# Hybrid decoder layer: the channel mixer's up projection in seven block products instead of eight, the down projection's running sums in DRAM

## The chip, the cores and the metric

The kernel runs on one core of one Trainium2 chip. Its time is device microseconds of one launch. The profile is one execution, taken by the hardware profiler; its times are microseconds (us) from the first instruction unless marked ns. The engines are PE (TensorE matmul), PEld (TensorE weight load), DVE (VectorE), ACT (ScalarE), POOL (GpSimd) and SP (SyncE, which here only issues DMAs).

## The reference

One decoder layer over 2048 tokens of 1024 features, in float32. A first part (a gated linear attention and a recurrent head group) ends in a residual stream x; the change leaves it alone. The second part is the channel mixer:

```python
h = modulate(x, norm_ffn_g, sh_f, sc_f)              # RMS norm, scale, shift
u = h @ w_up                                         # 1024 -> 5632 columns
up = pad(u, 2 tokens in front)
u = sum(conv_w[j] * up[:, j:j + T] for j in range(3)) + conv_b
gate, val = split(u, 2)                              # 2816 columns each
x = x + gt_f * ((silu(gate) * val) @ w_down)         # 2816 -> 1024
out = rms_norm(x, final_g)
```

## The kernel before

Features lie on the 128 partitions and tokens on the free axis. Tokens go in four blocks of 512. Phase 1 computes the first part. Phase 2 is the channel mixer: it takes two token blocks at a time (a pass; HB = 2, so there are two passes), and in each pass goes over the 22 pairs of a gate tile and a value tile, of 128 hidden features each.

Every float32 matrix product is made of three matmuls on rounded operands: a tensor t is split into hi (a copy that rounds, on ScalarE) and lo = t - hi (a subtraction on VectorE or GpSimd), and the product is hi·hi + hi·lo + lo·hi. A matmul takes 128 features of weights (128x128) against 512 tokens. `gemm3` (L276 to L278) sums the eight blocks of 128 features of one tile and one token block in a PSUM bank: 24 matmuls. `Weights` loads and splits weights (L179 the hi part on ScalarE; L182 the lo part, on GpSimd for every third piece and on VectorE otherwise).

For a tile, `conv_tile` runs `gemm3` for both token blocks, copies the bank to SBUF (`ub`, L1121), and applies the three taps (L1123 to L1125, with the last two tokens of the block before in `ccar`). `hidden` makes silu(gate)·value of two such tiles and splits it (`hh`, `hl`, L1151 and L1152). After a group of four or five hidden tiles (`kgroups`), `down` multiplies them into the 8 output tiles of both blocks (L1162 to L1164) and adds to `acc`, 16 tiles that stay in SBUF for the whole pass (L1167). `finish` normalises the output.

`stage_h` makes a block's operands: 8 tiles, each loaded from `x2d`, scaled (L265), rounded (L266) and subtracted (L267). The operands of the first two blocks are made where phase 1 ends, beside the last steps of the recurrent state's chain (the `rw_` and `rs_` tiles); those of the next two blocks, and the last block's output projection (`d3`, 192 matmuls), at the end of the first pass.

The order of each engine's instructions is fixed when the program is built, by a scheduler that goes by priorities (the order of the code) and by its own estimate of when inputs are ready and buffers free. Each engine then runs its list in order and waits at semaphores. All DMAs are issued from SP's list.

## Time and profile before

| | |
|---|---|
| time, median of 3 runs | 2974.28 us (2970.91 to 2977.05) |
| span of the profiled execution | 2964.6 us |
| PE busy | 2835.6 us (96%) |
| DVE busy | 1879.8 us (63%) |
| ACT busy | 1290.3 us (44%) |
| POOL busy | 735.9 us (25%) |
| mean granted clock of TensorE | 0.975 of full speed |

The span runs from the first to the last instruction. The profiled execution has no time of its own beside its span; the median of the runs lies 9.7 us above the span, which is what lies around it. Busy shares are means over phases with different limits. A matmul's duration overlaps with its neighbours' (they are pipelined), so its rate is read from the distance of two starts. The engine's idle time counts where others wait for it.

### The profile page before, as it was taken

Reading aid. Unit: us, or ns where it says so; the run is one execution under the profiler, and the core shown is the slowest. Engines: PE = TensorE matmul, PEld = TensorE weight load, DVE = VectorE, ACT = ScalarE, POOL = GpSimd, SP = SyncE. Lnnn points to the kernel's source line nnn. Section 1 sums busy time; section 2 is a strip of 40 time slices with the busy share of each in tenths; the row PEclk is TensorE's granted clock in tenths of the full one; section 3 lists DMA queues with packets and bytes.
Section 4 is the critical chain, followed back from the end, with each engine's and each line's share of the span. In section 5 each row is a group of like instructions: output and inputs, shape, how many; then the busy total and the mean of one; then the engine's idle time right before and its main releaser. Section 6 shows DMA issues by size and latency. Waiting matters only on the chain.

```text
span 2964.6 us, 53912 instructions
## 1 busy us (share of the span) xinstructions
PE 2835.6 (96%) x20824; PEld 2310.7 (78%) x20824; DVE 1879.8 (63%) x3877; ACT 1290.3 (44%) x2625; POOL 735.9 (25%) x995
## 2 busy tenths in 40 slices
...
GB/s 280 166 169 191 159 122 136 150 143 117 118 104 109 105 113 150 144 141 105 180 63 55 44 53 42 55 38 62 98 152 161 45 52 38 61 36 56 52 36 79
DMA packets 250050, 309.61 MB, mean 104 GB/s; under 512 B 68160, under 2 KB 139072, under 8 KB 249792
## 3 DMA queue, kind: packets, MB, share of 16 engines
...
q8 instruction: 164, 2.69, 0.4%
...
## 4 chain that ended last, share of the span: by engine, by line
PE 69%; DVE 10%; DMA 5%; ACT 3%; issue 2%; POOL 0%; SPq 0%; DVEq 0%; ACTq 0%; POOLq 0%
PE g_bank L276 13%; PE g_bank L277 13%; PE g_bank L278 13%; PE g_bank L1162 5%; PE g_bank L1164 5%; PE g_bank L1163 5%; DMA w_st<-in_ada_t 1%; PE gl_bank L690 1%; DVE w_lo L182 1%; DMA inv_a<-rw_mab 1%; DVE rw_pr L893 1%; DVE rw_t L832 1%; PE g_bank L444 1%; PE g_bank L442 1%; PE g_bank L443 1%
## 5 line engine op out<-in xcount | busy, mean ns | idle before, releaser
L276 PE MATMUL g_bank<-h_hi,w_hi 128*128 128x512 f32 x2144 | 846.3, 395 | 6.9 <-ACT carry L331 3.6
L277 PE MATMUL g_bank<-h_lo,w_hi 128*128 128x512 f32 x2144 | 844.9, 394 | 1.5 <-DVE h_lo L267 1.5
L278 PE MATMUL g_bank<-h_hi,w_lo 128*128 128x512 f32 x2144 | 844.2, 394 | 0.4 <-DVE w_lo L182 0.4
L179 ACT CAST w_hi<-w_st 128x512 fp32r<-128x512 f32 (+2 forms) x424 | 306.1, 725 | 533.3 <-PE g_bank L1163 310.3
L276 PEld LDWEIGHTS g_bank<-h_hi,w_hi 128*128 128x128 f32 x2144 | 405.3, 189 | 94.6 <-ACT carry L331 4.7
L277 PEld LDWEIGHTS g_bank<-h_lo,w_hi 128*128 128x128 f32 x2144 | 406.0, 189 | 85.8 <-DVE h_lo L267 2.1
L278 PEld LDWEIGHTS g_bank<-h_hi,w_lo 128*128 128x128 f32 x2144 | 405.6, 189 | 85.8 <-DVE w_lo L182 0.9
L182 POOL TENSOR_TENSOR w_lo<-w_st,w_hi 128x512 fp32r<-128x512 f32 (+2 forms) x141 | 228.2, 1619 | 696.0 <-ACT w_hi L179 648.2
L182 DVE TENSOR_TENSOR w_lo<-w_st,w_hi 128x512 fp32r<-128x512 f32 (+2 forms) x283 | 247.0, 874 | 144.0 <-ACT w_hi L179 135.9
L1124 DVE SCALAR_TENSOR_TENSOR cv<-ub,vt,cv 128x512 f32<-128x512 f32 x176 | 151.7, 862 | 229.2 <-ACT cv L1123 226.1
L1167 DVE SCALAR_TENSOR_TENSOR acc<-g_bank,mod,acc 128x512 f32<-128x512 f32 (+1 forms) x168 | 120.9, 723 | 240.1 <-PE g_bank L1164 240.1
L1163 PE MATMUL g_bank<-hl,w_hi 128*128 128x512 f32 x640 | 250.7, 392 | 0.0
L1164 PE MATMUL g_bank<-hh,w_lo 128*128 128x512 f32 x640 | 249.8, 392 | 0.0
L1162 PE MATMUL g_bank<-hh,w_hi 128*128 128x512 f32 x640 | 248.5, 392 | 0.0
L1126 POOL COPY ccar<-ub 128x2 f32<-128x2 f32 x176 | 66.5, 378 | 535.7 <-ACT ub L1121 535.4
L1121 ACT COPY ub<-g_bank 128x512 f32<-128x512 f32 x176 | 102.5, 583 | 103.5 <-PE g_bank L278 94.4
L1151 ACT CAST hh<-th 128x512 fp32r<-128x512 f32 x88 | 54.6, 621 | 209.3 <-DVE th L1147 209.3
L1163 PEld LDWEIGHTS g_bank<-hl,w_hi 128*128 128x128 f32 x640 | 120.1, 188 | 27.0
L1164 PEld LDWEIGHTS g_bank<-hh,w_lo 128*128 128x128 f32 x640 | 120.1, 188 | 27.1
L1162 PEld LDWEIGHTS g_bank<-hh,w_hi 128*128 128x128 f32 x640 | 120.2, 188 | 26.8
L1125 DVE SCALAR_TENSOR_TENSOR cv<-ub,vt,cv 128x512 f32<-128x512 f32 x176 | 134.4, 764 | 5.9
L1123 ACT ACTIVATE cv<-g_bank,vt 128x512 f32<-128x512 f32 x176 | 138.1, 784 | 0.0
...
## 6 DMA issues: line engine op xcount, KB each, us to landing
...
w_st<-in_w_in SPq DMA_DIRECT2D x168, 256.0 KB, 2.9
proj<-ev SPq DMA_DIRECT2D x100, 256.0 KB, 2.9
w_st<-in_ada_t SPq DMA_DIRECT2D x64, 256.0 KB, 3.5
x_k<-in_x SPq DMA_DIRECT2D x48, 256.0 KB, 3.5
w_st<-in_w_out SPq DMA_DIRECT2D x48, 256.0 KB, 3.2
w_st<-in_ffn_down SPq DMA_DIRECT2D x48, 256.0 KB, 2.6
...
```

Of the source, the lines that this page charges most:

```text
L179: A.copy(out=hi[:, 0:w], in_=t[:, 0:w])
L182: eng.tensor_tensor(out=lo[:, 0:w], in0=t[:, 0:w], in1=hi[:, 0:w].bitcast(F32), op=ALU.subtract)
L276: PE.matmul(out=ps, lhsT=wh, rhs=hi, start=k == 0, stop=False)
L277: PE.matmul(out=ps, lhsT=wh, rhs=lo, start=False, stop=False)
L278: PE.matmul(out=ps, lhsT=wl, rhs=hi, start=False, stop=k == KT - 1)
L1123: A.activation(out=cv, in_=ps, func=AF.Identity, scale=vt[:, o_cw + 88 + t:o_cw + 89 + t], bias=vcol("conv_b", t))
L1124: V.scalar_tensor_tensor(out=cv, in0=ub[:, 1:NB + 1], scalar=vt[:, o_cw + 44 + t:o_cw + 45 + t], in1=cv, op0=ALU.mult, op1=ALU.add)
L1125: V.scalar_tensor_tensor(out=cv, in0=ub[:, 0:NB], scalar=vt[:, o_cw + t:o_cw + t + 1], in1=cv, op0=ALU.mult, op1=ALU.add)
L1162: PE.matmul(out=ps, lhsT=wh, rhs=hh, start=j == 0, stop=False)
L1163: PE.matmul(out=ps, lhsT=wh, rhs=hl, start=False, stop=False)
L1164: PE.matmul(out=ps, lhsT=wl, rhs=hh, start=False, stop=j == n - 1)
L1167: V.scalar_tensor_tensor(out=a_, in0=ps, scalar=mod[:, 40 + ft:41 + ft], in1=a_, op0=ALU.mult, op1=ALU.add)
```

## The change

The up projection of a pass is a product of two by two blocks: the rows are the gate tile and the value tile, the inner dimension is cut into a lower and an upper half of 512 features, and the columns are the pass's two token blocks. Eight block products of 12 matmuls became seven (Strassen's scheme in Winograd's form). The weights are a11, a12 (gate, lower and upper features) and a21, a22 (value); the operands b11, b21 are the first block's halves, b12, b22 the second's. For every pair of tiles GpSimd makes four sums of weights (s1, s2, a21 + a11, s2 + a12), and seven pieces are split instead of the two tiles. The operand sums t1 to t4 are made once in a pass, by `operands_b`. The products collect in two banks: x is read four times while products are still added to it, and z twice. The value tile comes out negated; its taps are negated to match (`ncw`). `up_a` makes the first block's gate tile (two products), `up_b` adds three products and yields the second block's value tile, and `up_c`, which is issued after the next pair's `up_a`, adds the last two.

The room that the operands need comes from `acc`: the running sums of the down projection now lie in DRAM (`accd`), and every group loads, adds and stores the 16 tiles through five buffers (`acct`). The groups of hidden tiles are one of two and five of four. The mask and constant tile `ct` moved to another pool without its first 128 columns, and a scratch of the DMA program is smaller. Up to the last steps of phase 1 the engines' lists are the same as before.

```diff
-    pools["np"], pools["nst"], pools["nhl"], pools["nev"], pools["nx"] = 1, 2, 3, 4, 4
+    pools["np"], pools["nst"], pools["nhl"], pools["nev"], pools["nx"] = 2, 8, 4, 6, 5
...
+    def either():
+        turn[0] += 1
+        return G if turn[0] % 3 == 0 else V
+    def split(t, pair):
+        hi, lo = pair
+        A.copy(out=hi, in_=t)
+        either().tensor_tensor(out=lo, in0=t, in1=hi.bitcast(F32), op=ALU.subtract)
...
+    def operands_b(b, hs):
...
+        def put(n_, t):
+            pair = hc(n_)
+            hs[n_].append(pair)
+            split(t, pair)
+        def whole(n_, k):
+            d = ubt()[:, 0:NB]
+            hi, lo = hs[n_][k]
+            either().tensor_tensor(out=d, in0=hi.bitcast(F32), in1=lo.bitcast(F32), op=ALU.add)
+            return d
+        for k in range(4):
+            two = []
+            for q in (k, k + 4):
+                xk = ubt()[:, 0:NB]
+                nc.sync.dma_start(out=xk, in_=x2d[b][:, q, :])
+                V.scalar_tensor_tensor(out=xk, in0=xk, scalar=mod[:, 32 + q:33 + q], in1=rb, op0=ALU.mult, op1=ALU.mult)
+                A.activation(out=xk, in_=xk, func=AF.Identity, bias=mod[:, 24 + q:25 + q])
+                two.append(xk)
+            b12, b22 = two
+            c = ubt()[:, 0:NB]
+            V.tensor_tensor(out=c, in0=b22, in1=b12, op=ALU.subtract)
+            put("t3", c)
+            b11 = whole("b11", k)
+            V.scalar_tensor_tensor(out=c, in0=c, scalar=-1.0, in1=b11, op0=ALU.mult, op1=ALU.subtract)
+            put("t2", c)
+            G.tensor_tensor(out=b12, in0=b11, in1=b12, op=ALU.subtract)
+            put("t1", b12)
+            put("b22", b22)
+            b21 = whole("b21", k)
+            V.scalar_tensor_tensor(out=c, in0=c, scalar=-1.0, in1=b21, op0=ALU.mult, op1=ALU.subtract)
+            put("t4", c)
+        return hs
...
+    def product(ps, t, ops, first, last):
+        wh, wl = parts_of(t)
+        for k in range(4):
+            c = slice(k * P, (k + 1) * P)
+            hi, lo = ops[k]
+            PE.matmul(out=ps, lhsT=wh[:, c], rhs=hi, start=first and k == 0, stop=False, skip_group_check=True)
+            PE.matmul(out=ps, lhsT=wh[:, c], rhs=lo, start=False, stop=False, skip_group_check=True)
+            PE.matmul(out=ps, lhsT=wl[:, c], rhs=hi, start=False, stop=last and k == 3, skip_group_check=True)
...
+    def up_a(j, hs):
+        u = {}
+        gw, vw = ffn_up[j], ffn_up[NH + j]
+        a11, a12, a21, a22 = (raw(w_[:, c * NB:(c + 1) * NB]) for w_ in (gw, vw) for c in range(2))
+        u["x"], w_ = gbank(), gbank()
+        product(u["x"], a11, hs["b11"], True, False)
+        s1, s2 = raw(), raw()
+        G.tensor_tensor(out=s1, in0=a21, in1=a22, op=ALU.add)
+        G.tensor_tensor(out=s2, in0=s1, in1=a11, op=ALU.add)
+        G.tensor_tensor(out=a21, in0=a21, in1=a11, op=ALU.add)
+        u["c11"] = ubt()
+        A.copy(out=u["c11"][:, 2:NB + 2], in_=u["x"])
+        product(w_, a12, hs["b21"], True, True)
+        V.tensor_tensor(out=u["c11"][:, 2:NB + 2], in0=w_, in1=u["c11"][:, 2:NB + 2], op=ALU.add)
+        u["w"] = (a12, a21, a22, s1, s2)
...
+    def up_b(u, hs):
+        a12, a21, a22, s1, s2 = u["w"]
+        product(u["x"], s2, hs["t2"], False, False)
+        u["c21"] = ubt()
+        A.copy(out=u["c21"][:, 2:NB + 2], in_=u["x"])
+        G.tensor_tensor(out=s2, in0=s2, in1=a12, op=ALU.add)
+        u["z"] = gbank()
+        product(u["z"], a21, hs["t3"], True, False)
+        product(u["x"], s1, hs["t1"], False, False)
+        u["c22"] = ubt()
+        A.copy(out=u["c22"][:, 2:NB + 2], in_=u["x"])
+        V.tensor_tensor(out=u["c22"][:, 2:NB + 2], in0=u["z"], in1=u["c22"][:, 2:NB + 2], op=ALU.add)
+    def up_c(u, hs):
+        a12, a21, a22, s1, s2 = u["w"]
+        product(u["x"], s2, hs["b22"], False, True)
+        u["c12"] = ubt()
+        A.copy(out=u["c12"][:, 2:NB + 2], in_=u["x"])
+        product(u["z"], a22, hs["t4"], False, True)
+        V.tensor_tensor(out=u["c21"][:, 2:NB + 2], in0=u["z"], in1=u["c21"][:, 2:NB + 2], op=ALU.add)
...
-            ps = gbank()
-            gemm3(ps, w, h)
...
-    kgroups = ((0, 5), (5, 10), (10, 14), (14, 18), (18, 22))
+    kgroups = ((0, 2), (2, 6), (6, 10), (10, 14), (14, 18), (18, 22))
...
+    def down_group(e, k0, k1, hid):
+        for ft in range(KT):
+            w = parts_of(raw(ffn_down[ft][:, k0 * P:k1 * P], (k1 - k0) * P), (k1 - k0) * P)
+            for i in range(HB):
+                b = e * HB + i
+                a_ = acct()
+                nc.sync.dma_start(out=a_, in_=x2d[b][:, ft, :] if k0 == 0 else accd[b][ft])
+                down(ft, w, hid, i, a_, b)
+                nc.sync.dma_start(out=accd[b][ft], in_=a_)
...
+        for j in range(NH):
+            u = up_a(j, hs)
+            if prev is not None:
+                up_c(prev[1], hs)
+                g = group_of[prev[0]]
+                hid[g].append(hidden(*prev))
+                if prev[0] == g[1] - 1:
+                    ready = g
+            up_b(u, hs)
+            while pending and j > 0:
+                finish(*pending.pop(0))
+            if ready is not None:
+                down_group(e, *ready, hid.pop(ready))
+                ready = None
+            prev = (j, u)
...
+            d3 = stage_d(NBLK - 1, prep_d(NBLK - 1), lp.tile([P, NB], F32, name="d_ss", tag="th", bufs=2))
+            h2 = operands_a((e + 1) * HB)
...
+                if ft == 3:
+                    operands_b((e + 1) * HB + 1, h2)
```

**VectorE where the channel mixer starts.** Before: `x_k` is a loaded tile of the second or first block, `h_lo` its operand, `rw_sv` the recurrent state.

```order
L265 SCALAR_TENSOR_TENSOR x_k<-x_k,mod,rbc 128x512 x4
L182 TENSOR_TENSOR w_lo<-w_st,w_hi 128x1024
L267 SCALAR_TENSOR_TENSOR h_lo<-x_k,mod,h_hi 128x512 x4
L265 SCALAR_TENSOR_TENSOR x_k<-x_k,mod,rbc 128x512
L182 TENSOR_TENSOR w_lo<-w_st,w_hi 128x1024
L1005 TENSOR_TENSOR rw_sv<-rs_bank,rw_sv 64x256 x2
L267 SCALAR_TENSOR_TENSOR h_lo<-x_k,mod,h_hi 128x512
L265 SCALAR_TENSOR_TENSOR x_k<-x_k,mod,rbc 128x512
L1006 TENSOR_TENSOR rw_sv<-rw_sv,rw_ec 64x256 x2
```

After, the second block's operands (`operands_b`): `ub` is scratch, `h_lo` the low part of one of t1, t2, t3, t4 and b22, `w_lo` a split weight.

```order
L1183 TENSOR_TENSOR ub<-ub 128x512
L1170 TENSOR_TENSOR ub<-h_hi,h_lo 128x512
L1139 TENSOR_TENSOR h_lo<-ub,h_hi 128x512
L1178 SCALAR_TENSOR_TENSOR ub<-ub,mod,rbc 128x512
L1186 SCALAR_TENSOR_TENSOR ub<-ub 128x512
L1139 TENSOR_TENSOR w_lo<-w_st,w_hi 128x512
L1031 TENSOR_SCALAR hn_rk<-rj_bank 128x8
L1139 TENSOR_TENSOR h_lo<-ub,h_hi 128x512
L1178 SCALAR_TENSOR_TENSOR ub<-ub,mod,rbc 128x512
L1139 TENSOR_TENSOR w_lo<-w_st,w_hi 128x512
L1183 TENSOR_TENSOR ub<-ub 128x512
L1139 TENSOR_TENSOR h_lo<-ub,h_hi 128x512
```

Two rows for a tile of 128 features became, for a pair of tiles (k and k + 4), two scalings, up to two sums of hi and lo (L1170), the differences (L1183, L1186, L1192) and up to five subtractions (L1139), a part of them on GpSimd. From the first scaling to the last of these operands VectorE's list has 79 rows' worth of instructions, 64 of them with 128x512 elements, and GpSimd's has 23 with 128x512 elements; TensorE's list has 72 matmuls of the up projection ahead of the last operand. At the end of the first pass the same list stands between the `rbc` of the fourth block and its last t operand: 57 VectorE instructions of 128x512, 20 of GpSimd, and 113 matmuls of 128x512.

**GpSimd in the middle of a pass.** Before: `ccar` and `ub` are the two carried tokens, `w_lo` split weights.

```order
L1120 COPY ub<-ccar 128x2 x2
L182 TENSOR_TENSOR w_lo<-w_st,w_hi 128x512
L1126 COPY ccar<-ub 128x2
L182 TENSOR_TENSOR w_lo<-w_st,w_hi 128x512
L182 TENSOR_TENSOR w_lo<-w_st,w_hi 128x1024
L1126 COPY ccar<-ub 128x2
L1120 COPY ub<-ccar 128x2 x2
```

After: `w_st` are raw weights and their sums.

```order
L1224 TENSOR_TENSOR w_st<-w_st 128x512
L1226 TENSOR_TENSOR w_st<-w_st 128x512
L1225 TENSOR_TENSOR w_st<-w_st 128x512
L1139 TENSOR_TENSOR w_lo<-w_st,w_hi 128x512
L1258 COPY ub<-ub 128x2
L1139 TENSOR_TENSOR w_lo<-w_st,w_hi 128x512
L1239 TENSOR_TENSOR w_st<-w_st 128x512
L1224 TENSOR_TENSOR w_st<-w_st 128x512
L1257 COPY ub<-ccar 128x2
L1259 COPY ccar<-ub 128x2
L1226 TENSOR_TENSOR w_st<-w_st 128x512
L1225 TENSOR_TENSOR w_st<-w_st 128x512
```

Between two groups of the down projection the list of TensorE now has 324 matmuls of the up projection in a row; beside them VectorE has 74 instructions of 128x512 (26 taps L1264 and L1265, 18 of the hidden tile L1277, L1278 and L1281, 17 splits, and 13 that read a PSUM bank), GpSimd 22 of 128x512 (13 sums of weights, 9 splits) and 21 copies of two columns. The 192 matmuls of a group follow nearly in one piece.

**SP in a group of the down projection.** Before: only weights are loaded (`acc` is loaded once, at a pass's first group).

```order
L174 DMA w_st<-in_ffn_up 128x1024
L174 DMA w_st<-in_ffn_down 128x640 x8
L174 DMA w_st<-in_ffn_up 128x1024 x10
L174 DMA w_st<-in_ffn_down 128x640 x8
L174 DMA w_st<-in_ffn_up 128x1024 x8
L174 DMA w_st<-in_ffn_down 128x512 x8
```

After: `acc` is a buffer, `acc_3` and the like a running sum in DRAM.

```order
L1330 DMA acc_3_18105<-acc 128x512
L1328 DMA acc<-acc_5_18115 128x512
L1330 DMA acc_3_18113<-acc 128x512
L1328 DMA acc<-acc_6_18108 128x512
L1330 DMA acc_4_18106<-acc 128x512
L1328 DMA acc<-acc_6_18116 128x512
L1330 DMA acc_4_18114<-acc 128x512
L1199 DMA w_st<-in_ffn_up 128x512
L1328 DMA acc<-acc_7_18109 128x512
```

A load and a store of 256 KB stand between the weights for each of the 16 tiles of a group. A store waits for VectorE's addition, and the loads behind it in the list wait with it.

## Rows read from the trace of the kernel before

**Rows 1.** Stretches of the span: each engine's busy time, clock and DMA.
```profile
core 0: us, PE busy (x) PEld busy (x) DVE busy (x) ACT busy (x) POOL busy (x), PEclk, DMA share, GB/s
1430.00:1440.00 10.00, 5.52 (x73) 4.61 (x73) 6.38 (x12) 4.30 (x7) 2.29 (x3) 0.92 0.40 133
1440.00:1450.00 10.00, 8.52 (x69) 6.35 (x71) 9.03 (x12) 4.69 (x9) 2.00 (x1) 0.56 0.75 249
1460.00:1470.00 10.00, 10.00 (x52) 8.43 (x51) 8.28 (x18) 2.89 (x4) 0.00 (x0) 1.00 0.48 143
1470.00:1480.00 10.00, 10.00 (x46) 8.29 (x45) 5.69 (x5) 5.99 (x9) 4.72 (x7) 1.00 0.99 341
1500.00:2900.00 1400.00, 1400.00 (x6176) 1154.86 (x6176) 715.13 (x916) 482.71 (x720) 240.34 (x402) 1.00 0.20 62
```

**Rows 2.** TensorE in order of time, both ends of 16 matmuls.
```profile
2893.26 0.39 PE L276 MATMUL g_bank<-h_hi,w_hi 128*128 128x512 f32 x1
...
2896.66 0.39 PE L276 MATMUL g_bank<-h_hi,w_hi 128*128 128x512 f32 x1
```

**Rows 3.** Groups of one shape, 1500 to 2900 us.
```profile
L1125 DVE SCALAR_TENSOR_TENSOR cv<-ub,vt,cv 128x512 f32<-128x512 f32 x168 | 126.2, 751 | 5.7
...
L1146 DVE SCALAR_TENSOR_TENSOR th<-th,cv 128x512 f32<-128x512 f32 x84 | 58.1, 692 | 62.6 <-ACT th L1145 62.6
...
L182 DVE TENSOR_TENSOR w_lo<-w_st,w_hi 128x512 fp32r<-128x512 f32 x27 | 19.5, 727 | 9.0 <-ACT w_hi L179 9.0
...
L182 POOL TENSOR_TENSOR w_lo<-w_st,w_hi 128x512 fp32r<-128x512 f32 x13 | 17.4, 1335 | 107.9 <-ACT w_hi L179 97.5 <-PE g_bank L1164 10.5
```

**Rows 4.** VectorE and GpSimd in order of time, 1475.5 to 1480.6 us.
```profile
1475.69 1.22 DVE L182 TENSOR_TENSOR w_lo<-w_st,w_hi 128x1024 fp32r<-128x1024 f32 x1
1475.84 1.12 POOL L1120 COPY ub<-ccar 128x2 f32<-128x2 f32 x1 [1.82 <-DVE cv L1125]
...
1477.58 2.40 POOL L182 TENSOR_TENSOR w_lo<-w_st,w_hi 128x1024 fp32r<-128x1024 f32 x1
1477.61 2.92 DVE L1125 SCALAR_TENSOR_TENSOR cv<-ub,vt,cv 128x512 f32<-128x512 f32 x1
```

**Rows 5.** Lines L1120, L1124 and L1167: shortest, median and longest in ns.
```profile
L1120 POOL COPY ub<-ccar x176: 184/185/1117, 1473.0 to 2896.5; 128x2 f32<-128x2 f32 x176
...
L1124 DVE SCALAR_TENSOR_TENSOR cv<-ub,vt,cv x176: 740/752/2277, 1474.2 to 2903.4; 128x512 f32<-128x512 f32 x176
...
L1167 DVE SCALAR_TENSOR_TENSOR acc<-g_bank,mod,acc x168: 468/750/752, 1565.4 to 2948.1; 128x512 f32<-128x512 f32 x152, 128x256 f32<-128x256 f32 x16
```

**Rows 6.** VectorE in order of time, where the channel mixer starts.
```profile
1435.91 2.74 DVE L265 SCALAR_TENSOR_TENSOR x_k<-x_k,mod,rbc 128x512 f32<-128x512 f32 x4 [3.06 <-ACT rbc L248]
...
1467.32 1.40 DVE L267 SCALAR_TENSOR_TENSOR h_lo<-x_k,mod,h_hi 128x512 fp32r<-128x512 f32 x2
```

**Rows 7.** Matmuls of L276, a third of the up products, by stretch.
```profile
1440.00:1450.00 10.00, 2.28 (x4) 1.32 (x4) 0.56 0.75 249
1450.00:1460.00 10.00, 3.98 (x11) 1.99 (x11) 1.00 0.48 150
1460.00:1470.00 10.00, 4.81 (x13) 2.35 (x13) 1.00 0.48 143
1470.00:1480.00 10.00, 5.45 (x14) 2.65 (x15) 1.00 0.99 341
1480.00:1490.00 10.00, 5.83 (x15) 2.69 (x15) 1.00 0.72 249
```

**Rows 8.** What TensorE waited for, 1480 to 2960 us.
```profile
PE rj_bank L232 <- DVE x_ss L257: 4.3, 1, 4.3
PE rj_bank L245 <- POOL rn L239: 1.1, 1, 1.1
```

**Rows 9.** DMA issues: KB each, median us to landing.
```profile
x<-xr SPq DMA_DIRECT2D x32, 256.0 KB, 2.3
...
acc<-x SPq DMA_DIRECT2D x32, 256.0 KB, 6.1
```

More of the change, by code (lines that the diff above doesn't have):

```diff
@@ L1111, in hybrid_kernel @@
     o_cw, _ = _VL["conv_w"]
[L1113 to L1126 removed]
+    ncw = lp.tile([P, 3, NH], F32, name="ncw", bufs=1)
@@ new lines, in raw, with parts_of @@
+    def raw(src=None, n=NB):
+        t = pools["w"].tile([P, NB], F32, name="w_st", tag="wst", bufs=pools["nst"])[:, 0:n]
+        if src is not None:
+            nc.sync.dma_start(out=t, in_=src)
+        return t
+    def parts_of(t, n=NB):
+        pair = [pools["w"].tile([P, NB], F32R, name=f"w_{s_}", tag=f"w{s_}", bufs=pools["nhl"])[:, 0:n] for s_ in ("hi", "lo")]
+        split(t, pair)
+        return pair
+    def product(ps, t, ops, first, last):
[6 more added lines that the diff above has]
+            PE.matmul(out=ps, lhsT=wl[:, c], rhs=hi, start=False, stop=last and k == 3, skip_group_check=True)
@@ L1154, in hidden, with down @@
         return out_
-    def down(ft, w, n, hid, i, a_, first, b, c=slice(0, NB)):
+    accd = [[dram.tile([P, NB], F32, name=f"acc_{b}_{ft}") for ft in range(KT)] for b in range(NBLK)]
+    def down(ft, w, hid, i, a_, b, c=slice(0, NB)):
+        n = len(hid)
         ps = gbank()[:, c]
@@ new lines, in stage_e @@
+        up_c(prev[1], hs)
+        k0, k1 = kgroups[-1]
+        hid = hid[kgroups[-1]]
+        hid.append(hidden(*prev))
+        n = k1 - k0
+        more = (e + 1) * HB < NBLK
+        sums = [lp.tile([P, NB], F32, name="x_ss", tag="fs", bufs=HB) for _ in bs_]
+        if more:
+            places = iter(["t2"] * 4 + ["t3"] * 4)
+            pools["pair"] = lambda: hc(next(places))
+            d3 = stage_d(NBLK - 1, prep_d(NBLK - 1), lp.tile([P, NB], F32, name="d_ss", tag="th", bufs=2))
+            h2 = operands_a((e + 1) * HB)
+            for ft in range(KT):
+                w = parts_of(raw(ffn_down[ft][:, k0 * P:k1 * P]))
+                for i, b in enumerate(bs_):
+                    a_ = acct()
+                    nc.sync.dma_start(out=a_, in_=accd[b][ft])
+                    down(ft, w, hid, i, a_, b)
+                    add_square(ap, sums[i], a_, ft == 0, V)
+                    nc.sync.dma_start(out=accd[b][ft], in_=a_)
+                if ft == 2:
```

175 lines of the change are left out of this document (86 added, 89 removed).

## The prediction

> **What bounds the kernel now.** I read the table of stretches first. From 1500 to 2900 us TensorE is busy for all of 1400 us at a granted clock of 1.00, while VectorE is busy for 715.13 us (51%), GpSimd for 240.34 (17%), and the DMA engines for a share of 0.20 [rows 1]. Next the waits: between 1480 and 2960 us TensorE waited for 4.3 and 1.1 us, both close to the end [rows 8]. So the channel mixer is bound by its matmuls, and one that goes is worth its issue distance. In order of time, 15 steps lead from 2893.26 to 2896.66 us, 0.2267 us each [rows 2].
>
> Then I looked at what the change leans on instead. A VectorE instruction of 128x512 with two SBUF inputs takes 0.69 to 0.75 us, GpSimd's subtraction of that size 1.335 us [rows 3]. The two engines get in each other's way. GpSimd started a subtraction at 1477.58 that took 2.40 us; VectorE's tap of 1477.61 took 2.92 us instead of 0.75 and ended 0.55 us after GpSimd's did. The other way round, a copy of two columns on GpSimd that started 0.15 us into a VectorE subtraction took 1.12 us [rows 4]; undisturbed it takes 185 ns, the median [rows 5]. L1124, two SBUF inputs, has a median of 752 ns and goes up to 2277; L1167, which reads a PSUM bank, never passes 752 (the same group).
>
> So where VectorE has two SBUF inputs, the two engines seem to take turns. The Trainium skill ("SBUF — State Buffer", section "Who interferes with whom") says so more sharply: the shared port pair is an exclusive lock, and VectorE's instructions with at most one SBUF input do not contend. Rows 4 and 5 agree with both.
>
> **Removed: the eighth product.** 22 pairs x 2 passes x 12 matmuls are 528, and they lie in the stretch without waits: 528 x 0.2267 = **-119.7 us**.
>
> **The start of the channel mixer.** Before, the operands of both blocks begin with L265 at 1435.91 us and end with L267 at 1468.72, after 32.8 us, with VectorE busy for 8.28 of 10 us [rows 6, 1]. TensorE was not held up much: it did 57 matmuls of L276, so 171 of the up projection, by 1490 us beside the end of phase 1 [rows 7], and goes on at 1/0.2267 a microsecond. After, VectorE has 64 instructions of full size in that chain, GpSimd 23, and TensorE's list has only 72 up matmuls ahead of the last operand. 64 x 0.727 are 46.5 us; at the busy share of 0.83 that is 56 us, and with some turns taken by GpSimd I put it at 60, so at 1496 us. Before had by then 171 + 6/0.2267 = 197 matmuls; 125 are missing: 125 x 0.2267 = **+28 us**. Bounds: at 0.79 us for each instruction (what fits the stretch of before) the chain ends after 50.6 us, with 155 done and 83 missing, +19; if all of GpSimd's 23 x 1.335 = 30.7 us come on top, after 81 us, 218 missing, +49. A chain in which TensorE pauses also costs clock: after ten us in which TensorE was busy for 5.52, 1440 to 1450 us shows 0.56 granted, a mixture of the levels 1.2 and 2.4 GHz [rows 1]. That is inside the upper bound.
>
> **The end of the first pass.** The same work for the next two blocks was hidden before (no wait there in rows 8). After, the fourth block's chain has 57 VectorE instructions, at 0.727 and a share of 0.83 again 50 us, with 113 matmuls of cover, 25.6 us: **+24 us**. Bounds: VectorE without gaps 41.4 us, +16; with GpSimd's 20 x 1.335 = 26.7 us on top, 68 us, +42.
>
> **The up projection between two groups.** 324 matmuls take 73.5 us. VectorE's instructions with two SBUF inputs are 26 taps x 0.751, 18 of the hidden tile x 0.692 and 17 splits x 0.727 = 44.3 us. GpSimd's are 22 x 1.335 = 29.4 us (the sums of weights are not in the trace; I take its subtraction of that size; a shorter one would only help B), and 21 copies at 0.185 undisturbed, 3.9 us. Together 77.6 us if the engines take strict turns, 4.1 more than TensorE's. VectorE's 13 instructions on PSUM banks lie beside GpSimd's. Some of the weight work of a stretch can run during the 46 us of the down group before it, as far as eight raw and four split buffers reach, so the loss is between 0 and 4.1 us; I take the middle, 2 us, for some ten stretches: **+20 us** (0 to 41). Below zero is excluded: TensorE waits for nothing here now. If nothing overlapped, another 13 x 0.75 = 9.8 us would come on top; that is rival C.
>
> ScalarE has 66 instructions a stretch, some 42 us by the kind of work it does before; it has room.
>
> **The down groups with sums in DRAM.** A group of four tiles moves 32 x 256 KB of sums, 8 x 256 KB of its weights and some 1 MB of the next, 11.5 MB, beside 204 matmuls (192 and 12 of the up projection), 46.2 us: 249 GB/s, and 341 have been seen [rows 1]. TensorE's share of time for one sum is 46.2/16 = 2.89 us, so five buffers allow 14.4 us for load, addition and store. A load took 2.3 us where the queue was quiet and 6.1 where 32 came together [rows 9]; a store of that size I take within the same two. 2.3 + 0.75 + 2.3 = 5.4 to 6.1 + 0.75 + 6.1 = 13 us: it fits, 0. The additions are the same ones as before. A group of two tiles has 108 matmuls, 24.5 us, for 10.5 MB, which at 341 GB/s take 30.8 us: 6.3 us late, twice. Part of it is loaded ahead: **+6 us** (0 to 13 by bytes). SP's list holds the loads behind each store, and those wait for VectorE's addition; the weights of the next pair are queued there as well, a risk that rival D prices.
>
> **The rest.** The end of the kernel reads a sum back from DRAM, 2.3 us, or not at all where the buffer is still there: 0, within 3. Phase 1 has the same lists: 0.
>
> **Sum.** -119.7 + 28 + 24 + 20 + 6 = -41.7 us on the profiled execution's span of 2964.6. The median, 2974.28, lies 9.7 us above it, and I carry that over: 2974.3 - 41.7 = **2932.6 us**.
>
> **The rivals.**
>
> *A, the forecast.* Both operand chains show, the port costs little. Its own range is 2895 to 2960: from below with both chains near the lower bound and the port at 0 (-119.7 + 19 + 16 + 6 = -79), above with the port at 4 us a stretch and the chains 10 us longer in all (-14). Chance 0.58.
>
> *B, the helpers keep up.* VectorE runs the chains without gaps and the port never binds. For: in the stretch to 2900 us VectorE and GpSimd together are busy for 955 of 1400 us. Against: 8.28 of 10 us was the share at the operands. -119.7 + 19 + 16 + 0 + 0 = -85, so 2890; with more cover for the second chain, down to 2870. Chance 0.17.
>
> *C, slower: the port binds in the up projection.* Mechanism: VectorE and GpSimd, each with its list in a fixed order, wait for each other's instruction nearly always, so that also the work on PSUM banks does not lie beside GpSimd's. Then a stretch takes 44.3 + 29.4 + 3.9 + 9.8 = 87.4 us instead of 73.5: +139 us over ten in place of the +20, so 2932.6 + 119 = **3050 us**. It decides from the point where a stretch loses 6.2 us (2 + 41.7/10), that is at 79.7 us. For: rows 4 and 5, and port demand that is already above TensorE's time. Against: VectorE's work on PSUM and the 46 us of each down group, where GpSimd has little to do, and only a part of the overlaps in the trace cost something. Turns for the instructions with two SBUF inputs alone make 77.6 us, so +41 over ten stretches and 2953 us, inside A. (By that page's lock, taken strictly, it is this 2953 and not 3050: a point against C.) Chance of C, with all between 2980 and 3050: 0.13.
>
> *D, the round trip of the sums paces the groups.* At 13 us for five buffers a sum takes 2.6 us; a group of two tiles has 24.5/16 = 1.53 for it, and loses 16 x 1.07 = 17 us, 34 for both instead of the 6, so 2961. For: 6.1 us a load when many are queued, and loads that stand behind stores. Against: 14.4 us of room in the ten groups of four. Chance 0.12.
>
> **How the numbers follow.** 0.2% of the time, 6 us, is what a measurement of this kernel can tell from no change. Faster by more: A and B nearly whole and most of D, 0.82; within it: the rim of A, D and C, 0.05; slower: C, 0.13. For the range I let go the lowest tenth, below 2880 (B's far half), and the highest, above 2985 (C's main part).
>
> **What would show it.** In the changed profile, TensorE should have 528 fewer matmuls at the same distance of 0.227 us and a clock of 1.00 in the up stretches. A gap of 20 to 50 us behind the end of phase 1, with `h_lo` or `ub` of VectorE or GpSimd as what ended it, and one of 15 to 40 us near the middle of the channel mixer show the two chains. Waits of TensorE for `w_lo` or for a PSUM bank that VectorE frees, 0 to 4 us a stretch, show the port; VectorE's taps should then often last over 1.2 us. In the down groups of two tiles a wait for VectorE's addition that itself waited for `acc` from DRAM shows the round trip; in those of four there should be none. I am wrong if the up stretches take 80 us or more, if the groups of four wait, or if neither chain leaves a gap.

## The result, and the profile after

The changed kernel takes **3052.04 us** (3042.04 to 3054.43, four runs) against 2972.89 of the kernel before on the same chips: a ratio of 1.026 (95% interval 1.024 to 1.029). It was forecast 42 us faster and is 79 us slower. The profiled span grew by 75.5 us, from 2964.6 to 3040.1. A run lasts 1.9 us longer than its own span (3042.04 against 3040.1), so most of the 9.7 us between median and span before, which the forecast carried over, are the difference between one execution and another. The time is nearly that of rival C, 3050; that rival's mechanism turns out to hold a part of it only. One of the four runs of e11, below, lasted 4226 us at a mean granted clock of 0.625 and is left out (the median is 2931.0 with it and 2928.6 without).

The table of stretches of the changed kernel, with the columns of [rows 1]: the start of the channel mixer, then an up stretch, a down group and the next up stretch, and the stretch behind the end of the first pass.

```profile
1480.00:1490.00 10.00, 2.08 (x8) 1.78 (x8) 8.12 (x14) 5.47 (x10) 1.73 (x1) 0.50 0.35 107
1490.00:1500.00 10.00, 2.81 (x4) 1.08 (x4) 9.94 (x10) 4.71 (x8) 7.17 (x5) 0.50 0.09 26
1572.20:1656.60 84.40, 81.85 (x355) 66.00 (x354) 69.65 (x90) 44.64 (x76) 43.74 (x45) 1.00 0.32 105
1656.60:1696.20 39.60, 39.60 (x176) 32.80 (x175) 14.86 (x21) 5.42 (x10) 7.99 (x8) 1.00 0.54 169
1696.20:1789.00 92.80, 83.06 (x354) 67.11 (x353) 65.70 (x87) 44.88 (x76) 42.50 (x44) 0.96 0.28 87
2264.30:2356.80 92.50, 71.46 (x271) 54.23 (x270) 86.23 (x101) 43.94 (x76) 55.81 (x46) 0.85 0.48 156
```

In [rows 1] TensorE had no idle microsecond from 1500 to 2900. Here a down group is still full (39.60 of 39.60), but the up stretch behind it is not: 92.8 us for 353 matmuls (the table counts the one that runs in from the stretch before as well), which need 80.0 at 0.2267 us. At 1490 TensorE is nearly empty, at half clock (0.50), while VectorE is full.

I count what a stretch loses as its length less its recorded matmuls times 0.2267 us. The ten up stretches lose 4.3, 12.8, 12.1, 13.2 and 12.5 in the first pass and 6.5, 12.6, 10.9, 15.4 and 6.7 in the second: **107 us**; those of before lose none. The start is counted by the 325th matmul of the channel mixer, up and down projection together: 1525.0 us before, 1572.2 now, **47 us**. From the end of the first pass's last whole stretch to the end of the second pass's first group **41 us** are lost. The eighth product gives -119.7. Together +75, as the span shows.

What TensorE waited for from 1430 us on, the three largest of its entries (engine, line and tile that waited, who let it go, us in total, times, longest); before there were two waits from 1480 us on, 5.4 us together [rows 8]:

```profile
PE g_bank L1214 <- POOL w_lo L1139: 37.6, 9, 8.2
PE g_bank L1212 <- ACT ub L1244: 36.0, 19, 5.3
PE g_bank L1212 <- ACT h_hi L1138: 20.8, 5, 7.9
```

One wait of the first kind, followed back through four engines. SP at the end of the down group of 1656 to 1696 us (L1328 loads a sum, L1330 stores one, L1199 loads weights), then GpSimd, TensorE and VectorE:

```profile
1694.38 0.32 SPq L1328 DMA_DIRECT2D acc<-acc  x1
1694.80 0.38 SPq L1330 DMA_DIRECT2D acc<-acc  x1
1697.97 0.32 SPq L1328 DMA_DIRECT2D acc<-acc  x1
1698.38 0.38 SPq L1330 DMA_DIRECT2D acc<-acc  x1
...
1711.99 0.32 SPq L1328 DMA_DIRECT2D acc<-acc  x1
1712.36 19.41 SPq L1199 DMA_DIRECT2D w_st<-in_ffn_up  x5
```

```profile
1715.46 1.26 POOL L1224 TENSOR_TENSOR w_st<-w_st 128x512 f32<-128x512 f32 x1 [13.14 <-DMA w_st<-in_ffn_up]
1716.66 0.18 POOL L1257 COPY ub<-ccar 128x2 f32<-128x2 f32 x1
1716.79 0.18 POOL L1259 COPY ccar<-ub 128x2 f32<-128x2 f32 x1
1716.92 1.26 POOL L1226 TENSOR_TENSOR w_st<-w_st 128x512 f32<-128x512 f32 x1
1718.14 1.25 POOL L1225 TENSOR_TENSOR w_st<-w_st 128x512 f32<-128x512 f32 x1
1719.36 1.26 POOL L1139 TENSOR_TENSOR w_lo<-w_st,w_hi 128x512 fp32r<-128x512 f32 x1
```

```profile
1720.67 0.79 PE L1214 MATMUL g_bank<-h_hi,w_lo 128*128 128x512 f32 x1 [7.40 <-POOL w_lo L1139]
1721.27 0.63 PE L1212 MATMUL g_bank<-h_hi,w_hi 128*128 128x512 f32 x1
1721.69 0.63 PE L1213 MATMUL g_bank<-h_lo,w_hi 128*128 128x512 f32 x1
```

```profile
1709.73 0.75 DVE L1265 SCALAR_TENSOR_TENSOR cv<-ub,ncw,cv 128x512 f32<-128x512 f32 x1
1720.78 0.75 DVE L1264 SCALAR_TENSOR_TENSOR cv<-ub,ncw,cv 128x512 f32<-128x512 f32 x1 [10.29 <-POOL ub L1258]
```

SP's loads of sums come some 3.5 us apart, where TensorE needs 2.72 us for a sum (twelve matmuls). The group's last matmul was at 1696.2; SP is through with the sums at 1712, and only then asks for the last weights of the next pair. GpSimd gets its first sum of weights going at 1715.46, then works off what is queued behind it, and TensorE has waited 7.40 us when `w_lo` is there. VectorE stands idle meanwhile, behind a copy of two columns in GpSimd's list. After the wait TensorE's matmuls come 0.43 us apart, at half clock (0.50 granted from 1720 to 1724 us), for seven matmuls, which costs some 1.7 us more; with two waits for L1244 of 2.3 us in all that is most of the 12.8 us that this stretch loses.

Four stretches of the first pass have such a wait, 7.1 to 8.2 us. In the second pass the same lateness comes to TensorE by another way, as the second kind of wait. At 2524.61 us GpSimd had waited 10.62 us for the weights of a sum, VectorE then 8.46 us for the copy L1258 behind the sums in GpSimd's list; so the hidden tile was late, ScalarE stood idle for it, and TensorE 5.30 us for the copy of a bank (L1244) behind that in ScalarE's list, the longest wait of that kind:

```profile
2533.76 0.62 ACT L1280 CAST hh<-th 128x512 fp32r<-128x512 f32 x1 [10.09 <-DVE th L1278]
```

What SP waited for from 1656 to 1713 us:

```profile
SPq L1328 <- DMA acc<-acc: 34.8, 15, 3.7
```

Fifteen loads waited for a DMA: the store just ahead of them in the list, which must have landed before its buffer is loaded again.

### The profile page after: what moved, and what is told of

Its sections match the earlier page's. It is cut to its first block, busy times and chain, and to the rows that moved or that the text cites. A ratio compares the mean times of both kernels' runs of the same rounds, so it can differ in the third digit from the quotient of the medians.

```text
span 3040.1 us, 54742 instructions
## 1 busy us (share of the span) xinstructions
PE 2776.1 (91%) x20296; PEld 2236.6 (74%) x20296; DVE 2136.3 (70%) x4248; ACT 1402.1 (46%) x2909; POOL 1102.1 (36%) x1193
## 5 line engine op out<-in xcount | busy, mean ns | idle before, releaser
L1212 PE MATMUL g_bank<-h_hi,w_hi 128*128 128x512 f32 x1232 | 500.2, 408 | 66.9 <-ACT ub L1244 36.0
L1214 PE MATMUL g_bank<-h_hi,w_lo 128*128 128x512 f32 x1232 | 491.4, 404 | 46.4 <-POOL w_lo L1139 37.6
L1213 PE MATMUL g_bank<-h_lo,w_hi 128*128 128x512 f32 x1232 | 495.7, 402 | 7.5 <-DVE h_lo L1139 4.7
L1138 ACT CAST w_hi<-w_st 128x512 fp32r<-128x512 f32 (+1 forms) x396 | 241.0, 609 | 522.6 <-PE g_bank L1296 292.2
L1139 POOL TENSOR_TENSOR w_lo<-w_st,w_hi 128x512 fp32r<-128x512 f32 (+1 forms) x132 | 193.5, 1466 | 416.0 <-ACT w_hi L1138 376.0
L1214 PEld LDWEIGHTS g_bank<-h_hi,w_lo 128*128 128x128 f32 x1232 | 239.8, 195 | 107.9 <-POOL w_lo L1139 41.7
L276 PE MATMUL g_bank<-h_hi,w_hi 128*128 128x512 f32 x736 | 297.5, 405 | 4.2 <-ACT carry L333 3.7
L1298 DVE SCALAR_TENSOR_TENSOR acc<-g_bank,mod,acc 128x512 f32<-128x512 f32 (+1 forms) x200 | 143.7, 727 | 217.8 <-PE g_bank L1297 179.9
L278 PE MATMUL g_bank<-h_hi,w_lo 128*128 128x512 f32 x736 | 296.0, 403 | 0.0
L277 PE MATMUL g_bank<-h_lo,w_hi 128*128 128x512 f32 x736 | 294.9, 401 | 0.0
L1139 DVE TENSOR_TENSOR w_lo<-w_st,w_hi 128x512 fp32r<-128x512 f32 (+1 forms) x264 | 198.3, 752 | 83.3 <-ACT w_hi L1138 83.0
L179 ACT CAST w_hi<-w_st 128x512 fp32r<-128x512 f32 x272 | 167.5, 618 | 125.6 <-PE g_bank L277 75.5
L182 POOL TENSOR_TENSOR w_lo<-w_st,w_hi 128x512 fp32r<-128x512 f32 x90 | 125.8, 1398 | 265.4 <-ACT w_hi L179 215.8
L182 DVE TENSOR_TENSOR w_lo<-w_st,w_hi 128x512 fp32r<-128x512 f32 x182 | 139.9, 769 | 75.7 <-ACT w_hi L179 64.1
L276 PEld LDWEIGHTS g_bank<-h_hi,w_hi 128*128 128x128 f32 x736 | 140.5, 191 | 36.6 <-ACT carry L333 4.7
L278 PEld LDWEIGHTS g_bank<-h_hi,w_lo 128*128 128x128 f32 x736 | 140.9, 191 | 30.2 <-issue 0.2
```

The costliest lines, as they stand in the source:

```text
L182: eng.tensor_tensor(out=lo[:, 0:w], in0=t[:, 0:w], in1=hi[:, 0:w].bitcast(F32), op=ALU.subtract)
L276: PE.matmul(out=ps, lhsT=wh, rhs=hi, start=k == 0, stop=False)
L277: PE.matmul(out=ps, lhsT=wh, rhs=lo, start=False, stop=False)
L278: PE.matmul(out=ps, lhsT=wl, rhs=hi, start=False, stop=k == KT - 1)
L1138: A.copy(out=hi, in_=t)
L1139: either().tensor_tensor(out=lo, in0=t, in1=hi.bitcast(F32), op=ALU.subtract)
```

## The experiments

"Lost" is what the ten up stretches lose, "start" the delay of the 325th matmul against 1525.0 us, "end" the loss around the end of the first pass, all in us from the profiled run. The ratio to the kernel before, run on the same chip, has its 95% interval. The runs come from several chips, on which the median of the kernel before went from 2966.8 to 2972.9 us: a difference of two medians from different chips is uncertain by some 6 us. e2, e3, e3n, e5 and e13 leave out work that the layer needs.

| run | median us | ratio to before | lost | start | end |
|---|---|---|---|---|---|
| changed kernel | 3052.0 | 1.026 (1.024 to 1.029) | 107 | 47 | 41 |
| e1 loads later | 3005.5 | 1.013 (1.009 to 1.016) | 55 | 55 | 46 |
| e2 no traffic of sums | 2996.1 | 1.010 (1.007 to 1.012) | 53 | 45 | 45 |
| e3 no weight sums | 2935.5 | 0.989 (0.987 to 0.992) | 8 | 38 | 37 |
| e3n the same, six raw buffers | 2939.7 | 0.990 (0.989 to 0.992) | 7 | 46 | 38 |
| e5 no t1 to t4 | 2997.0 | 1.010 (1.007 to 1.012) | 89 | 31 | 30 |
| e6 operands on VectorE | 3035.0 | 1.023 (1.021 to 1.025) | 95 | 40 | 47 |
| e10 weight sums on VectorE | 3025.8 | 1.020 (1.018 to 1.022) | 84 | 44 | 46 |
| e8 = e1 and e10 | 2954.5 | 0.995 (0.994 to 0.997) | 14 | 53 | 42 |
| e9 = e8 and e6 | 2937.4 | 0.990 (0.989 to 0.992) | 15 | 38 | 35 |
| e11 = e9, no GpSimd splits | 2928.6 | 0.986 (0.984 to 0.988) | 6 | 46 | 33 |
| e12 = e11, first groups free | 2918.6 | 0.984 (0.982 to 0.986) | 6 | 30 | 34 |
| e13 = e12, short operand sums | 2910.3 | 0.980 (0.977 to 0.982) | 6 | 32 | 26 |

**e1: loads of sums later in SP's list.** Each load is queued behind the store three sums before it (in a pass's last group as well, not shown).

```diff
+    stores = []
+    def load_sum(a_, src):
+        ld = nc.sync.dma_start(out=a_, in_=src)
+        if len(stores) >= 3:
+            (order only: ld behind stores[-3] in SP's list)
...
-                nc.sync.dma_start(out=a_, in_=x2d[b][:, ft, :] if k0 == 0 else accd[b][ft])
+                load_sum(a_, x2d[b][:, ft, :] if k0 == 0 else accd[b][ft])
                 down(ft, w, hid, i, a_, b)
-                nc.sync.dma_start(out=accd[b][ft], in_=a_)
+                stores.append(nc.sync.dma_start(out=accd[b][ft], in_=a_))
```

> The load of a running sum is put in SP's list behind the store of the sum three places before it, instead of right behind the store that frees its own buffer (five before); nothing else changes. Theory Q (SP's queue): in the trace of the changed kernel SP waits in each group of four 15 times, 34.8 us in all, for the store just issued, turns at 3.4 us a sum instead of TensorE's 2.7 and is 12 us late with the next pair's weights; TensorE then waits 7 to 8 us and goes on at half clock. Without that, eight stretches lose 4 instead of 12 us: about 64 us, 2985 us (2965 to 3000), and the waits for POOL w_lo L1139 of 7 to 8 us are gone. Theory P (the shared port, rival C): 3052 within 8. Theory M (the memory round trip itself is too long): additions wait for loads that now come later, 3060 or more.

It took 47 us off, and the waits of 7 to 8 us are gone; in the three stretches of the second pass that had lost 10.9 to 15.4 us none over 2.2 us is left. SP in a group of four, then an up stretch of that run:

```profile
1692.13 0.32 SPq L1337 DMA_DIRECT2D acc<-acc  x1
1692.50 0.42 SPq L1324 DMA_DIRECT2D acc<-acc  x1
1694.85 0.32 SPq L1337 DMA_DIRECT2D acc<-acc  x1
1695.22 0.42 SPq L1324 DMA_DIRECT2D acc<-acc  x1
```

```profile
1829.80:1914.40 84.60, 81.72 (x355) 65.96 (x354) 68.03 (x87) 44.63 (x76) 43.83 (x44) 1.00 0.22 68
```

The stores (L1337) now come 2.72 us apart, TensorE's own pace. Theory Q holds for the waits, P as the whole cause and M fall. The gain is smaller than the 64 us expected, and 3005.5 lies above the range of Q: some 5 us a stretch are left (55 in ten), and the start and the end lose 8 and 5 us more than they did.

**e2: no traffic of sums.** In the groups between a pass's first and last, additions go into the last five buffers of `acct`.

```diff
-                a_ = acct()
-                nc.sync.dma_start(out=a_, in_=x2d[b][:, ft, :] if k0 == 0 else accd[b][ft])
+                if k0 == 0:
+                    kept.append(acct())
+                    nc.sync.dma_start(out=kept[-1], in_=x2d[b][:, ft, :])
+                a_ = kept[-1 if k0 == 0 else -1 - (ft * HB + i) % 5]
                 down(ft, w, hid, i, a_, b)
-                nc.sync.dma_start(out=accd[b][ft], in_=a_)
+                if k0 == 0:
+                    nc.sync.dma_start(out=accd[b][ft], in_=a_)
```

> Loads and stores of the running sums are left out in all groups of a pass but its first and last; additions go into five buffers that stay (so the sums are not the reference's). Theory Q: SP's list then holds only weights there, the seven stretches behind such groups lose 4 instead of 12 us, some 56 to 80 us less: 2972 to 2996. Theory P: the same work on VectorE and GpSimd, 3052 within 8.

2996: at the upper edge of what Q said, and 53 us lost in the up stretches, against 55 in e1. So bytes and round trips to DRAM cost the up stretches nothing beyond their order in SP's list.

**e3 and e3n: no weight sums; and with six raw buffers.** The four additions go, s1 is a11 and s2 is a22; e3n has `nst` 6 instead of 8.

```diff
-        s1, s2 = raw(), raw()
-        G.tensor_tensor(out=s1, in0=a21, in1=a22, op=ALU.add)
-        G.tensor_tensor(out=s2, in0=s1, in1=a11, op=ALU.add)
-        G.tensor_tensor(out=a21, in0=a21, in1=a11, op=ALU.add)
+        s1, s2 = a11, a22
...
-        G.tensor_tensor(out=s2, in0=s2, in1=a12, op=ALU.add)
```

> GpSimd's four sums of weights for each pair are left out (176 x 1.3 us = 229 us of GpSimd); the products use unsummed weights. Theory P: the port is relieved by 13 x 1.3 = 17 us in each stretch, which then runs at TensorE's pace: 80 to 110 us less, 2940 to 2970. Theory Q: the weights still come late behind the sums' stores; TensorE is spared only the three sums behind the late load, 3.8 us: 8 x 4 = 30 less, about 3020, with waits for w_lo in the same eight places.

> As the run without weight sums (2936), but with six raw buffers for weights instead of eight, so that beside a pair's four there are two spare ones, as many as the changed kernel has beside its six. In the run with eight SP was as late as before (the last load of a sum 16 us behind the last matmul of its group), yet the stretches lost 0.6 us. Theory B (the eight raw buffers hid the late loads; it is the two buffers that the sums occupy that let SP's lateness through): the waits of 7 us come back in eight places, 40 to 60 more than 2936, so 2975 to 2996. Theory W (GpSimd's work is what was late): 2936 within 8.

e3 came out at 2936, better than P expected, and took away Q's loss as well, though SP still waited in the group of 1644 to 1684 us as long as in the changed kernel:

```profile
SPq L1324 <- DMA acc<-acc: 34.6, 14, 4.3
```

So late loads alone do no harm; they harm together with the sums. In e3's stretch behind that group no engine waits for a load of weights, and VectorE's longest wait for GpSimd is 3.2 us; in the changed kernel GpSimd waited there 13.14 us for a load, and VectorE 10.29 behind it. That the two spare buffers were the link, theory B, is wrong as I put it: e3n is at 2940. Without the sums a raw piece is also free again as soon as it is split, which neither run separates.

**e10 and e8: weight sums on VectorE, old and later order.** Four times in `up_a` and `up_b`:

```diff
-        G.tensor_tensor(out=s1, in0=a21, in1=a22, op=ALU.add)
+        V.tensor_tensor(out=s1, in0=a21, in1=a22, op=ALU.add)
```

> The run with the later loads (3005) and, besides, the weight sums on VectorE instead of GpSimd. Theory P2 (what is left, 4.5 to 6 us a stretch, is turns at the port: 13 sums hold it for 1.3 us each on GpSimd and 0.69 on VectorE): a stretch needs the port for 44.3 + 9.0 + 12.0 + 3.9 = 69.2 us instead of 77.6, under TensorE's 73.5, and loses 1 or less: 10 x 4.5 = 45 less, 2960 (2950 to 2975). Theory V (VectorE's own busy time is what is left): it gets 9 us more work in a stretch, 3005 or more.

> The changed kernel with its weight sums on VectorE and SP's order as it was (each load of a running sum right behind the store that frees its buffer): the fourth corner beside 3052 (GpSimd, old order), 3005 (GpSimd, later loads) and 2954 (VectorE, later loads). Theory Q' (the late weights cost the same whichever engine sums them, since all four pieces must be there before the third product): 47 more than 2954, about 3000, with waits of 5 to 8 us in eight places. Theory W' (the late weights cost only because GpSimd's four instructions of 1.3 us come behind them; VectorE does the three first ones in 2.1 us): 2954 to 2970.

With e1 these are the four corners: 3052 (GpSimd, old order), 3026 (VectorE, old order), 3005 (GpSimd, later loads), 2955 (VectorE, later loads). The order alone is worth 47 us, the engine alone 26, both 97.5 (42, 21 and 94 if each kernel is taken against the kernel before on its own chip): each hides part of the other. In e8 a stretch loses 1.4 us on the mean, where P2 said 1 or less. In e10 the order costs 71 us, more than Q' expected, and W' falls: the late weights cost whichever engine adds them. The long wait in an up stretch of e10, 7.4 us as in the changed kernel but let go by ScalarE's rounding:

```profile
PE g_bank L1212 <- ACT w_hi L1138: 7.4, 1, 7.4
```

What the port does in e1, in the lists of VectorE, GpSimd and ScalarE in order of time, and TensorE where it waits:

```profile
1865.53 1.78 DVE L1139 TENSOR_TENSOR w_lo<-w_st,w_hi 128x512 fp32r<-128x512 f32 x1
...
1869.22 1.78 DVE L1264 SCALAR_TENSOR_TENSOR cv<-ub,vt,cv 128x512 f32<-128x512 f32 x1
...
1876.64 0.68 DVE L1139 TENSOR_TENSOR w_lo<-w_st,w_hi 128x512 fp32r<-128x512 f32 x1
```

```profile
1865.01 1.75 POOL L1225 TENSOR_TENSOR w_st<-w_st 128x512 f32<-128x512 f32 x1
...
1868.65 1.81 POOL L1139 TENSOR_TENSOR w_lo<-w_st,w_hi 128x512 fp32r<-128x512 f32 x1 [1.29 <-ACT w_hi L1138]
```

```profile
1872.90 0.62 ACT L1280 CAST hh<-th 128x512 fp32r<-128x512 f32 x1 [2.52 <-DVE th L1278]
...
1876.42 0.58 ACT L1244 COPY ub<-g_bank 128x512 f32<-128x512 f32 x1
```

```profile
1877.05 0.50 PE L1212 MATMUL g_bank<-h_hi,w_hi 128*128 128x512 f32 x1 [1.64 <-ACT ub L1244]
```

VectorE's 0.68 us become 1.78 beside GpSimd's instructions, as in [rows 4]. VectorE is late with the hidden tile (L1278), ScalarE waits 2.52 us for it, and behind that in ScalarE's list stands the copy of a bank (L1244) that the next product adds to. That is how the port reaches TensorE.

**e5: no t1 to t4.**

```diff
-            c = ubt()[:, 0:NB]
-            V.tensor_tensor(out=c, in0=b22, in1=b12, op=ALU.subtract)
...
+            put("t3", b12)
+            put("b22", b22)
+        hs["t1"] = hs["t2"] = hs["t3"]
+        hs["t4"] = hs["b22"]
```

> The operand sums t1 to t4 and the whole values they need are left out: t1 and t2 use t3's buffers filled with b12, t4 those of b22, so the second block's operands cost eight splits. Theory L (length of the chain): the two gaps, 44 us at the start of the channel mixer and 44 at the end of the first pass, are VectorE's and GpSimd's work on these operands; without it 60 to 80 us go, 2972 to 2992. Theory K (the gaps come from other causes: the clock, DMAs, the state's last steps): at most 20 less, 3032 or more.

55 us less, under the 60 to 80 of theory L and over the 20 of K: inconclusive. By the table the start gained 16 us and the end 11; the other 18 came from the up stretches, where nothing was left out. The edit also moved work in the fixed order (the first up matmul came at 1462.7 instead of 1443.9), and the start still lost 31 us.

**e6 and e9: operands of the second block on VectorE alone**, by itself and on top of e8.

```diff
-            split(t, pair)
+            split(t, pair, V)
...
-            either().tensor_tensor(out=d, in0=hi.bitcast(F32), in1=lo.bitcast(F32), op=ALU.add)
+            V.tensor_tensor(out=d, in0=hi.bitcast(F32), in1=lo.bitcast(F32), op=ALU.add)
...
-            G.tensor_tensor(out=b12, in0=b11, in1=b12, op=ALU.subtract)
+            V.tensor_tensor(out=b12, in0=b11, in1=b12, op=ALU.subtract)
```

> All work on the second block's operands that GpSimd did (23 instructions of 128x512 at the start, 20 at the end of the first pass) is put on VectorE. Theory E (turns at the port: each of GpSimd's instructions holds VectorE for about 1.3 us, VectorE needs 0.69 for the same): each gap shorter by some 0.6 x 20 = 12 us, 3028 (3015 to 3040). Theory F (the engines work beside each other): each gap longer by 20 x 0.69 = 14 us, 3080.

> The run with the weight sums on VectorE and, besides, the second block's operands on VectorE alone. Theories P2 and E together: 2960 - 24 = 2936 (2920 to 2950), faster than the kernel before. Theories V or F: 3005 and more.

More instructions on the engine that was full made both kernels faster, 17 us each: theory E, not F. For e9 both medians are of one chip; e6 gains 13 if each kernel is taken against the kernel before on its own chip, and the intervals of its ratio and of the changed kernel's just overlap. In the first gap it is plain (47 to 40, and 53 to 38); in the second, e6 lost 6 us more and e9 7 less, so there it is not settled.

**e11 and e12: no splits on GpSimd; and the loads of x in a pass's first group free to go ahead.**

```diff
-        return G if turn[0] % 3 == 0 else V
+        return V
```

```diff
-        if len(stores) >= 3:
+        if late and len(stores) >= 3:
...
+                load_sum(a_, x2d[b][:, ft, :] if k0 == 0 else accd[b][ft], k0 > 0)
```

> The run with sums and operands on VectorE (2937) and, besides, no split of weights on GpSimd any more: only its copies of two columns stay. Theory E (turns): 9 splits a stretch and those beside the operand chains hold the port 1.3 us each, VectorE needs 0.69; VectorE's list in a stretch is then 53 + 6 + 10 = 69 us, under TensorE's 73.5; the chains are 4 us shorter each: 2925 to 2932. Theory V (VectorE is now what is short, 69 of 73.5 leaves no room in a fixed order): the stretches lose 2 to 4 us again, 2945 to 2970.

> The run without GpSimd splits (2931), but the later place of the loads holds only in the groups of four tiles; in a pass's first group of two tiles the loads (of x) may go ahead as in the changed kernel. Theory R (in a group of two tiles a sum has only 1.4 us, so a load three sums ahead comes too late: in the run of 2931 these two groups lose 10.0 and 6.5 us, TensorE waiting for additions, and 3.5 and 4.1 in the changed kernel): 6 to 9 us less, 2922 to 2925. Theory S (the groups of two are held by VectorE's saturated list, not by their loads): 2931 within 4.

e11 came out as theory E said. e12 gained 10 us instead of 6 to 9: the first pass's group of two loses 3.1 us instead of 10.0, as R said, the second's 6.0 instead of 6.5, so R holds for one of them. The start, in which the first pass's group of two is counted, lost 16 us less; the order moved there as well (the 73rd up matmul at 1493 instead of 1503 us). e12 is the fastest kernel that computes the whole layer: **2918.6 us**, 1.6% under the kernel before (1.4 to 1.8). An up stretch of it has no idle time left:

```profile
1675.10:1756.40 81.30, 81.30 (x358) 66.83 (x357) 70.00 (x109) 45.14 (x76) 10.98 (x21) 1.00 0.23 72
```

VectorE has 109 instructions here where the changed kernel had 87, and is busy for 70.00 us against 65.70: 22 more cost 4.3 us, since the others are no longer stretched (the tap L1264 on `vt` takes 746 ns there on the mean, 1069 in the changed kernel's stretch of 1696 to 1789 us).

**e13: short operand sums**, on e12.

```diff
-            V.tensor_tensor(out=d, in0=hi.bitcast(F32), in1=lo.bitcast(F32), op=ALU.add)
+            V.tensor_tensor(out=d[:, 0:8], in0=hi[:, 0:8].bitcast(F32), in1=lo[:, 0:8].bitcast(F32), op=ALU.add)
```

(and the same for t1, t2 and t4)

> The run of 2919, but 20 of VectorE's instructions in each operand chain (the whole values of b11 and b21 and the sums t1, t2, t4) work on 8 of 512 columns: they cost some 0.1 instead of 0.69 us, and the rest of t1, t2 and t4 is left out. All else, the splits too, stays. Theory L (what is left of the two gaps, 30 us at the start and 35 at the end of the first pass, is the length of VectorE's chain): 20 x 0.6 = 12 us less in each, 2919 - 24 = 2895 (2888 to 2902). Theory K (the gaps are held by loads, ScalarE or the state's last steps): 2919 within 6.

8 us less (13 if each is taken against the kernel before on its own chip), between the theories. The second gap shrank by 8 us, as L wants; the first did not: its 73rd up matmul came at 1493.1 us as in e12 (1493.2). VectorE now has pauses there, the longest of them 2.58 us for a DMA of the first part, so what holds the last 30 us of the start is open.

## Why the prediction was wrong, point by point

**The eighth product** was right. The page counts 20824 PE instructions before and 20296 after, 528 fewer, and in an undisturbed part of the changed kernel six steps take 1.36 us, still 0.227 each:

```profile
1711.30 0.39 PE L1212 MATMUL g_bank<-h_hi,w_hi 128*128 128x512 f32 x1
...
1712.66 0.39 PE L1212 MATMUL g_bank<-h_hi,w_hi 128*128 128x512 f32 x1
```

**The start and the end of the first pass** were right in kind and short in size: 47 us (forecast 28, bounds 19 to 49) and 41 (24, bounds 16 to 42). Both lie at the upper bound, where all of GpSimd's work comes on top of VectorE's, and not where I put them. The first chain's ends, the answer to [rows 6]:

```profile
1433.81 3.39 DVE L1151 SCALAR_TENSOR_TENSOR ub<-ub,mod,rbc 128x512 f32<-128x512 f32 x5
...
1459.81 0.68 DVE L1139 TENSOR_TENSOR h_lo<-ub,h_hi 128x512 fp32r<-128x512 f32 x1
1460.41 1.76 DVE L1178 SCALAR_TENSOR_TENSOR ub<-ub,mod,rbc 128x512 f32<-128x512 f32 x1
1462.09 1.76 DVE L1186 SCALAR_TENSOR_TENSOR ub<-ub 128x512 f32<-128x512 f32 x1
...
1509.02 0.68 DVE L1139 TENSOR_TENSOR h_lo<-ub,h_hi 128x512 fp32r<-128x512 f32 x1
```

75.9 us instead of 60, and the 73rd up matmul came at 1510.4, right behind that, as the order said. GpSimd was not only at the operands: the weight sums of the first pairs ran there too, which the sum left out. With GpSimd's operands on VectorE the start lost 7 us less (e6 against the changed kernel) and 15 less (e9 against e8), so turns with GpSimd are a part of it; they are not shown for the rest.

**The up projection between groups** is the term that failed: 107 us instead of 20. Two causes were in it. The turns at the port were priced at 4.1 us a stretch, halved to 2; e1, with SP's lateness gone, shows 55 us in ten stretches, above the upper bound of 41, and e8, e9 and e11 bring them to 14, 15 and 6 by taking work from GpSimd. The half that was to be done ahead, beside the down groups, did not show. Shortest, median and longest of a tap in the changed kernel, for [rows 5]:

```profile
L1264 DVE SCALAR_TENSOR_TENSOR cv<-ub,vt,cv x88: 736/752/1835, 1506.5 to 2981.1; 128x512 f32<-128x512 f32 x88
```

The Trainium skill ("SBUF — State Buffer", section "Who interferes with whom") calls the port pair that VectorE and GpSimd share an exclusive lock, and has VectorE's instructions with two SBUF inputs contend with those of GpSimd that read SBUF. Taken strictly, that is an estimate of 77.6 - 73.5 = 4.1 us a stretch and 41 in ten; e1 measured 55, so the rule was worth more than the half that I kept of it.

**The groups of four with sums in DRAM** were priced at 0, and that step hid the larger cause. The groups themselves lose nothing, as forecast. The other 52 us of the up stretches (107 less the 55 of e1) began here, and TensorE paid them one stage later. The step asked whether five buffers leave 14.4 us for a round trip, and they do. It did not ask how long SP's list is blocked: a load that stands right behind the store of its own buffer makes the queue wait for the landing, 34.8/15 = 2.3 us on the mean, so a sum takes SP some 3.5 us where TensorE needs 2.72, and 16 sums leave it 12 to 13 us late. I had seen both, the loads behind each store and the weights in the same list, and put the price in rival D on the groups of two, not on the stretch behind the groups of four. The landing itself was in the bounds, for [rows 9]:

```profile
acc<-acc SPq DMA_DIRECT2D x352, 256.0 KB, 3.1
```

**The groups of two** lost 3.5 and 4.1 us (counted in the start and the end above), 7.6 where 6 was forecast; the 34 of rival D did not come.

**Rival C** had the time, 3050, for a reason that holds a part, so its number is luck. It put 139 us of turns at the port into the up stretches. They lose 107, of which e1 leaves 55 when SP is on time. What that is short of 139 the two gaps make up for, which came out 36 us longer than the 28 and 24 that C took over from the forecast. Its assumption that nothing of VectorE lies beside GpSimd was too strong: work on a PSUM bank was not held up, for L1298, the addition to a sum, never passes 753 ns. The order of SP's list is worth 47 us with the weight sums on GpSimd and 71 with them on VectorE, the engine 26 or 51.

One sum of the forecast is off by a little: the terms of A's upper end add up to -11.7 us, 2963, and not to -14.

What stays open: whether late loads cost nothing without weight sums because the sums are gone or because a raw piece is free again sooner, and what bounds the last 30 us of the start.
